# Strassen block products in the gated product of a two-layer trunk, with weight sums on VectorE and GpSimd

## Chip, cores and metric

The kernel runs on one core of a Trainium2 chip. TensorE (PE in the profile) multiplies, VectorE (DVE), ScalarE (ACT) and GpSimd (POOL) work elementwise, SyncE (SP) issues most DMAs. The metric is the device time of one execution in microseconds (us); lower is better. Each engine takes its instructions in an order of its own, and engines wait for one another by semaphores.

## What is computed

Two layers on an input of 256 positions by 2048 channels, float32. The first layer (a Mamba-2 mixer beside block-sparse attention) isn't touched. The second is a diagonal state-space mixer, and the change sits in its gated product, the line with `w_glu`:

```python
def s5_mixer(x, w_in, lam_re, ..., w_glu, w_out):
    u, gate = jnp.split(x @ w_in, 2, axis=-1)
    y = jax.nn.gelu(s5_ssm(u, lam_re, lam_im, log_dt, b_re, b_im, c_re, c_im, d_skip))
    ga, gb = jnp.split(y @ w_glu, 2, axis=-1)
    y = ga * jax.nn.sigmoid(gb)
    return (y * jax.nn.silu(gate)) @ w_out
...
        x = layer_norm(DEEPNORM_ALPHA * x + h, ln_g[layer], ln_b[layer])
```

Here `y` is 256 x 2048 and `w_glu` 2048 x 4096.

## The kernel before

**Products.** Every operand is split into a high and a low part, and a product takes three terms: high by high, high by low, low by high (xmm, L297 to L304). Weights come in units of two K tiles (128 rows each) by 512 columns, 512 KB: split_to loads a unit (L242, SP's queue, tile "raw"), ScalarE copies it to the rounded high half (L248, "wh"), VectorE subtracts to get the low half (L253, "wl"). Each of these tiles has four buffers, and split_to runs three units ahead of the matmuls, so the copy of unit n can start only when the matmuls of unit n - 4 are done. A unit is 2 K tiles x 2 halves of the 256 positions x 3 terms = 12 matmuls of 128x512.

**Gated product.** The 4096 columns are cut into 8 chunks of 512 (256 of ga, the matching 256 of gb), each of 16 K tiles, 8 units, 96 matmuls into two PSUM banks ("main"), one for each half of the positions. Two pairs of banks alternate. The operand is y5, the scan's output, whose K tiles lie in slot "A" in high and low form. Chunks 0 and 1 are made together by product_pair (L376): six units of chunk 0, six of chunk 1, then `between` (which finishes the scan's remaining jobs), then the last two units of chunk 0 (units 12 and 13 of the pair) and of chunk 1 (14 and 15). This is so because the last quarter of y5 comes late: y_load(3) (L1403, a reload from DRAM on GpSimd's DMA queue) and y_split(3) (L1413 and L1414) stand right ahead of it. The other six chunks follow one by one (`product`).

**After a chunk.** glu_jobs queues a gate job and a turn job. Gate: sigmoid of the gb half out of PSUM (L1455, ScalarE), product with the ga half (L1457, VectorE, twice 256 columns), product with the silu gate sg1 (L1458). Turn: four transposes on TensorE (L463 in a helper, tile "turn"), then the high and low halves of the next operand y2 (L1466 ScalarE, L1467 VectorE) in slot "C". Jobs are spread over the units that follow (pump, L282), and each one is held behind the splits of the unit two further on (run, L267).

**Around it.** Ahead stands the state-space scan, whose short matmuls and elementwise work are mixed into products with x1; it uses tiles of a pool (`w1`). Behind stands the output product with y2 (`wo1`), the residual with x1, and the layer norm. The order of instructions on each engine is worked out when the kernel is built, from the order of the code, these holds and the tile framework's scheduler.

## Time and profile before

| what | us |
|---|---|
| median of 3 runs (lowest to highest) | 1319.52 (1318.27 to 1320.66) |
| span of the profiled execution | 1316.6 |
| TensorE busy in it | 1310.0 |
| VectorE, ScalarE, GpSimd busy | 963.7, 695.5, 320.1 |
| gated product and what is mixed into it | about 1040 to 1229 |
| one chunk of it (96 matmuls, 4 transposes) | 22.23 |

In the rows of the profile a line such as `L253 DVE TENSOR_TENSOR wl<-raw,wh 128x1024 fp32r<-128x1024 f32 x430 | 532.8, 1243 | 284.1 <-ACT wh L248 282.1` gives the line of the code, the engine, the operation, the tile written and those read, shapes, the count, busy us in all, mean ns of one, idle us ahead of them on that engine, and who ended most of that idle time. In a timeline the first two numbers of a row are its start and its duration in us, x3 says that three instructions are merged, and the brackets give the idle time ahead and who ended it. Duration rows overlap a little, since an instruction begins before the one ahead has drained.

### The profile page before, as it was taken

The numbers are of one execution on the slowest core, as the hardware profiler recorded it, in microseconds if no ns is written. First come the engines' busy times: TensorE is split into PE (matmuls) and PEld (weight loads), VectorE is DVE, ScalarE is ACT, GpSimd is POOL, SyncE is SP. The second block draws the span as 40 slices with busy tenths as digits, with TensorE's granted clock in tenths as the row PEclk, the third lists the DMA queues.
The fourth block names the chain that finished last, engine by engine and source line by source line (L and its number), as shares of the span: only waits on it lengthen the run. The fifth ranks groups of instructions, "written<-read, shape, count | busy, mean of one in ns | idle before, by whom it ended". The sixth has DMA issues, their size and how long they took to land.

```text
span 1316.6 us, 21451 instructions
## 1 busy us (share of the span) xinstructions
PE 1310.0 (99%) x7999; PEld 1101.0 (84%) x7999; DVE 963.7 (73%) x1612; ACT 695.5 (53%) x946; POOL 320.1 (24%) x615
## 2 busy tenths in 40 slices
PE   9999999999999999999999999999999999999998
PEld 9988888878888888888888888888888888888885
DVE  6778977875786876777798765858998855555565
ACT  6566668865644554654654444444446544444441
POOL 0043000111045535236788300023232000000000
PEclk9999999999999999999999999999999999999999
DMA  8555566565556567666656868479998665555761
GB/s 318 181 181 178 187 208 194 192 206 176 175 177 239 200 217 230 203 207 225 229 201 231 285 219 312 153 246 320 332 288 311 211 217 191 189 192 188 255 224 68
DMA packets 96638, 288.33 MB, mean 219 GB/s; under 512 B 18994, under 2 KB 29186, under 8 KB 96020
## 3 DMA queue, kind: packets, MB, share of 16 engines
q1 hardware_dynamic: 75796, 245.05, 55.2%
q0 software_dynamic: 6336, 28.35, 6.3%
q10 hardware_dynamic: 14400, 13.54, 3.2%
q8 instruction: 63, 1.03, 0.3%
q14 instruction: 43, 0.35, 0.1%
HBM read 264.35 MB, written 21.00 MB: 217 GB/s over the span
## 4 chain that ended last, share of the span: by engine, by line
PE 99%; DVE 0%; ACT 0%; issue 0%
PE main L302 62%; PE main L358 17%; PE main L359 9%; PE main L325 3%; PE aux L463 2%; PE aux L917 1%; PE aux L818 1%; PE enc L1336 1%; PE dec L1381 1%; PE aux L1035 1%; PE aux L1003 1%; PE main L405 1%; PE dec L1377 0%; PE turn L463 0%; PE aux L472 0%; PE aux L1002 0%
## 5 line engine op out<-in xcount | busy, mean ns | idle before, releaser
L253 DVE TENSOR_TENSOR wl<-raw,wh 128x1024 fp32r<-128x1024 f32 x430 | 532.8, 1243 | 284.1 <-ACT wh L248 282.1
L248 ACT ACTIVATE wh<-raw 128x1024 fp32r<-128x1024 f32 x430 | 453.7, 1059 | 495.3 <-PE main L302 265.2
L302 PE MATMUL main<-wh,A 128*128 128x512 f32 x1536 | 488.0, 394 | 0.0
L302 PEld LDWEIGHTS main<-wh,A 128*128 128x128 f32 x1536 | 287.4, 188 | 59.5 <-issue 0.5
L302 PE MATMUL main<-wl,A 128*128 128x512 f32 x768 | 300.6, 391 | 0.0
L358 PE MATMUL main<-A,wh 128*128 128x512 f32 x768 | 272.7, 399 | 0.0
L302 PE MATMUL main<-wh,C 128*128 128x512 f32 x832 | 262.6, 393 | 0.0
L359 PE MATMUL main<-A,wl 128*128 128x256 f32 x768 | 215.3, 280 | 0.0
L302 PEld LDWEIGHTS main<-wh,C 128*128 128x128 f32 x832 | 155.7, 188 | 33.1
L358 PEld LDWEIGHTS main<-A,wh 128*128 128x128 f32 x768 | 144.2, 188 | 34.9 <-ACT b L890 0.4
L302 PEld LDWEIGHTS main<-wl,A 128*128 128x128 f32 x768 | 144.3, 188 | 28.7 <-issue 0.2
L302 PE MATMUL main<-wl,C 128*128 128x512 f32 x416 | 162.2, 390 | 0.0
L359 PEld LDWEIGHTS main<-A,wl 128*128 128x128 f32 x768 | 145.0, 189 | 0.4 <-issue 0.2
L742 POOL TENSOR_TENSOR c<-c 128x8 f32<-128x8 f32 (+2 forms) x192 | 96.0, 518 | 27.4 <-DMA wb<-c 19.9
L302 PEld LDWEIGHTS main<-wl,C 128*128 128x128 f32 x416 | 78.1, 188 | 16.1
L358 PE MATMUL main<-C,wh 128*128 128x512 f32 x192 | 68.3, 400 | 0.0
L925 POOL TENSOR_TENSOR ssq<-ssq,c 128x256 f32<-128x256 f32 x16 | 18.2, 1138 | 163.3 <-ACT c L923 162.7
L359 PE MATMUL main<-C,wl 128*128 128x256 f32 x192 | 53.5, 281 | 0.0
L744 POOL TENSOR_TENSOR c<-c,c 128x4 f32<-128x4 f32 (+2 forms) x96 | 49.2, 513 | 7.4
L976 POOL TENSOR_TENSOR b<-b 128x128 f32<-128x128 f32 x16 | 8.3, 518 | 172.2 <-DVE b L975 169.8
L745 POOL TENSOR_TENSOR c<-c,c 128x4 f32<-128x4 f32 (+2 forms) x96 | 47.2, 491 | 0.0
L358 PEld LDWEIGHTS main<-C,wh 128*128 128x128 f32 x192 | 36.0, 188 | 8.6
(298 smaller groups left out, 1344.4 us busy)
## 6 DMA issues: line engine op xcount, KB each, us to landing
raw<-in_wi SPq DMA_DIRECT2D x270, 512.0 KB
raw<-in_wo SPq DMA_DIRECT2D x96, 512.0 KB
raw<-in_wglu SPq DMA_DIRECT2D x64, 512.0 KB
wt<-wb POOLq DMA_DIRECT2D x16, 896.0 KB, 8.3
wb<-ob ACTq DMA_DIRECT2D x16, 512.0 KB
b<-cumd SPq DMA_DIRECT2D x16, 256.0 KB
bc<-in_s5bc SPq DMA_DIRECT2D x16, 256.0 KB
wb<-c POOLq DMA_DIRECT2D x16, 256.0 KB, 3.6
```

The costliest lines, as they stand in the source:

```text
L248: high = A.activation(wh, raw, AF.Copy)
L253: splits[n] = (loaded[-1], high, V.tensor_tensor(wl, raw, wh.bitcast(F32), op=OP.subtract))
L302: end = T.matmul(ps[o], l[:, k, sl], r[:, j, :], start=start and i == 0, stop=stop and i == 2)
L325: T.matmul(pv[o // 2][:, o % 2, :], l[:, j, sl], r[:, k, :], start=first and i == 0 and o % 2 == 0, stop=end and i == 2 and o % 2 == 1, sk ...
L358: T.matmul(ps[o], wh[:, j, sl], xx[:, k, :, :].rearrange("p a n -> p (a n)"), start=first, stop=False, skip_group_check=True)
L359: lastmm[:] = [T.matmul(ps[o][:, S : 2 * S], wl[:, j, sl], xh[:, k, :], start=False, stop=end, skip_group_check=True)]
L405: lastmm[:] = [T.matmul(pv[o // 2][:, o % 2, :], l[:, n, sl], r[:, k, :], start=at == 0 and l is wh and i == 0 and o % 2 == 0, stop=False, ...
L463: end = T.transpose(dst[:, i * P : i * P + P], s, ident)
L742: G.tensor_tensor(p[:, :, :, 0:m], cs[:, :, :, 1 : m + 1], cs[:, i, :, n : n + 1].unsqueeze(1).to_broadcast([P, 2, 4, m]), op=OP.mult)
L744: G.tensor_tensor(cs[:, 0, :, n + 1 : n + 1 + m], p0[:, 0, :, 0:m], p1[:, 1, :, 0:m], op=OP.subtract)
L745: G.tensor_tensor(cs[:, 1, :, n + 1 : n + 1 + m], p0[:, 1, :, 0:m], p1[:, 0, :, 0:m], op=OP.add)
L925: G.tensor_tensor(ssq, ssq, jk[:, f, :], op=OP.add)
```

## The change

Chunks 0 and 1 stay as they were. Chunks 2 to 7 are made in three pairs. In a pair, of the 16 K tiles six (0, 1, 2 and 4, 5, 6) are multiplied by Strassen's scheme in Winograd's form: the 2x2 blocks are the two halves of the positions by the two sets of three K tiles on one side, and the two sets of K tiles by the two chunks on the other. Seven products of 3 K tiles x 3 terms = 9 matmuls take the place of eight. The ten other K tiles are added as ordinary units (n1 for one chunk, n2 for the other) into the same PSUM banks, so a pair has 7 x 9 + 10 x 12 = 183 matmuls, where it had 2 x 96 = 192.

- The weight blocks a, b, c, d of a pair (128 x 1536 each, 768 KB) are loaded on SP's queue into tiles "sraw" (four buffers). Three sums t1, t2, t4 are made by VectorE in one more buffer, t3 by GpSimd in place. split_fast splits the seven operands into "sh" (ScalarE) and "sl" (VectorE), two buffers each.
- The operand sums of y5 (n1, n2, s3, n4) are made once, in `between`: two quarters of y are reloaded from DRAM (GpSimd's queue) into two buffers of "sraw", GpSimd adds, ScalarE and VectorE split.
- The block products p1, q5, v2, q7, p2, p4, p3 run in the order of `flow`, mixed with the units n1 and n2. Partial results are copied out of PSUM (copy, less, out1, out2).
- A gate then works on a whole chunk in SBUF: sigmoid on ScalarE, product with sg1 on GpSimd, the last product on VectorE (glu_whole).
- The tiles for this lie in a pool "gp", which is opened when the scan's pool "ws" is closed, in `between`. sg1 moves to slot "D", where x1 was; x1 is stored to DRAM (xkeep) ahead of the scan and reloaded behind the gated product.
- The bytes of weights loaded don't change. PSUM banks: the pair's first bank names X and Y are those of chunk 0 for the first pair, Z and R those of chunk 1.

Where lines are new, the numbers of the code after are used: L302 becomes L365, L248 L312, L253 L317, L1455 L1534, L1457 L1536, L1458 L1537, L1413 and L1414 L1481 and L1482.

```diff
+Q = 3
+KA = [0, 1, 2]
+KB = [4, 5, 6]
+KC = [3, 7, 8, 9, 10, 11, 12, 13, 14, 15]
+GROUPS = 3
...
+        flow = ["p1", "q5", "n2", "v2", "n2", "q7", "n2", "p2", "n1", "n2", "p4", "n1", "n2", "p3", "n1", "n1", "n1"]
+        fast = {}
+        before = {}
+        nc1 = len(KC) // 2
+        for g in range(GROUPS):
+            seen = {"n1": nc1, "n2": 0}
+            base = len(units)
+            for i, s in enumerate(flow):
+                if s in seen:
+                    units.append(io["wgc"][2 * nc1 * g + seen[s]])
+                    seen[s] += 1
+                else:
+                    fast[base + i] = (g, {"p1": "a", "q5": "t", "v2": "t", "q7": "b", "p2": "d", "p4": "t", "p3": "c"}[s])
+                    units.append(None)
+            at0 = {s: base + flow.index(s) for s in ("p1", "q5", "v2", "q7", "p4")}
+            for n, what in ((at0["p1"] - 1, ("load", "a")), (at0["p1"] - 1, ("load", "b")), (at0["p1"], ("load", "c")),
+                            (at0["q7"], ("load", "d")), (at0["p1"], ("sum", "t1")), (at0["q5"], ("sum", "t3")),
+                            (at0["v2"] - 1, ("sum", "t2")), (at0["p4"] - 1, ("sum", "t4"))):
+                before.setdefault(n, []).append((g,) + what)
...
+        gpool = []
+        blocks = {}
+
+        def block(g, name):
+            blocks[g, name] = gpool[0].tile([P, Q, 512], F32, tag="sraw", bufs=4, name=nm("sraw"))
+            return blocks[g, name]
+
+        def prepare(g, kind, name):
+            if kind == "load":
+                ins = nc.sync.dma_start(block(g, name).rearrange("p k n -> p (k n)"), io["wgs"][g, "abcd".index(name)])
+                blocks[g, name, "load"] = ins
+                loaded.append(ins)
+            elif name == "t1":
+                V.tensor_tensor(block(g, "t"), blocks[g, "a"], blocks[g, "b"], op=OP.add)
+            elif name == "t3":
+                G.tensor_tensor(blocks[g, "b"], blocks[g, "b"], blocks[g, "c"], op=OP.add)
+            else:
+                V.tensor_tensor(blocks[g, "t"], blocks[g, "t"], blocks[g, {"t2": "c", "t4": "d"}[name]], op=OP.add)
+
+        def split_fast(n):
+            raw = blocks[fast[n]]
+            wh = gpool[0].tile([P, Q, 512], F32R, tag="sh", bufs=2, name=nm("sh"))
+            high = A.activation(wh, raw, AF.Copy)
+            wl = gpool[0].tile([P, Q, 512], F32R, tag="sl", bufs=2, name=nm("sl"))
+            low = V.tensor_tensor(wl, raw, wh.bitcast(F32), op=OP.subtract)
+            splits[n] = (loaded[-1], high, low)
+            ready[n] = (wh, wl)
 
         def split_to(i):
             while nsplit[0] <= min(i, len(units) - 1):
                 n = nsplit[0]
+                for what in before.get(n, ()):
+                    prepare(*what)
+                if n in fast:
+                    split_fast(n)
+                    nsplit[0] += 1
+                    continue
...
+            scan = l1.enter_context(ExitStack())
+            ws = scan.enter_context(tc.tile_pool(name="ws", bufs=2))
 
             def w1(tag, shape, bufs=2, dt=F32):
-                return wk.tile(shape, dt, tag=tag, bufs=bufs, name=nm(tag))
+                return (wk if tag in ("p1", "gt") else ws).tile(shape, dt, tag=tag, bufs=bufs, name=nm(tag))
+
+            xkeep = dram.tile([P, 2, D], F32, name="xkeep")
+            jobs.append(lambda: nc.gpsimd.dma_start(xkeep, x1))
...
-            sg1 = wk.tile([P, 2, D], F32, tag="sg1", bufs=1, name="sg1")
+            sg1 = big("D", [P, 2, D])
...
+            def glu_whole(cc, j):
+                d = {}
+
+                sb, t1 = cc[:, :, 256:512], cc[:, :, 0:256]
+                d["t"] = t1
+
+                def gate():
+                    A.activation(sb, sb, AF.Sigmoid)
+                    G.tensor_tensor(sb, sb, sg1[:, :, 256 * j : 256 * j + 256], op=OP.mult)
+
+                def mix():
+                    V.tensor_tensor(t1, t1, sb, op=OP.mult)
+
+                return [gate, rest, mix, lambda: glu_turn(d, j)]
...
+            def between():
+                finish()
+                scan.close()
+                gpool.append(l1.enter_context(tc.tile_pool(name="gp", bufs=1)))
+                ops = gpool[0].tile([P, 4, 2, Q, P], F32R, name="ops")
+                xo["c1"] = gpool[0].tile([P, 2, 512], F32, name="c1")
+                ys = [gpool[0].tile([P, 4, S], F32, tag="sraw", bufs=4, name=nm("yr")) for _ in range(2)]
+                for i in range(2):
+                    nc.gpsimd.dma_start(ys[i], yd[i].rearrange("g a c -> (g a c)").rearrange("(f p t) -> p f t", p=P, t=S))
+
+                def tok(i, t):
+                    return ys[i].rearrange("p f (s t c) -> p t f s c", s=4, t=2)[:, t, 0:Q]
+
+                def put(name, i, tag, a, b, op):
+                    def go():
+                        a_, b_ = (xo[v, "r"] if isinstance(v, str) else tok(*v) for v in (a, b))
+                        r = xo[name, "r"] = w1(tag, [P, 2, 256]).rearrange("p a n -> p (a n)")[:, 0 : Q * P].rearrange("p (f s c) -> p f s c", f=Q, s=4)
+                        G.tensor_tensor(r, a_, b_, op=op)
+                        h, l = (ops[:, i, n].rearrange("p f (s c) -> p f s c", s=4) for n in range(2))
+                        A.activation(h, r, AF.Copy)
+                        V.tensor_tensor(l, r, h.bitcast(F32), op=OP.subtract)
+                        xo[name] = ops[:, i, 0], ops[:, i, 1]
+                    return go
+
+                jobs.extend([put("n1", 0, "gt", (0, 1), (1, 1), OP.subtract), put("n2", 1, "p1", "n1", (0, 0), OP.subtract),
+                             put("s3", 2, "gt", (0, 0), (0, 1), OP.subtract), put("n4", 3, "p1", "n2", (1, 0), OP.add)])
...
+                def copy(name, tag, ps):
+                    def go():
+                        e[name] = w1(tag, [P, 2, 256]).rearrange("p a n -> p (a n)")
+                        A.activation(e[name], ps, AF.Copy)
+                    return go
+
+                def less(o):
+                    A.activation(c2[:, o, :], X, AF.Copy)
+                    G.tensor_tensor(c2[:, o, :], e["z5"], c2[:, o, :], op=OP.subtract)
+
+                def out2():
+                    for o, ps in enumerate((Z, R)):
+                        V.tensor_tensor(c2[:, o, :], ps, c2[:, o, :], op=OP.add)
+
+                def out1():
+                    V.tensor_tensor(c1[:, 0, :], Y, e["p1"], op=OP.add)
+                    A.activation(c1[:, 1, :], X, AF.Copy)
+
+                made = {"p1": (X, lambda: whole(KA, 0), True, [copy("p1", "p1", X)]), "q5": (Y, lambda: summed("n1"), True, [copy("z5", "gt", Y)]),
+                        "v2": (X, lambda: summed("n2"), False, [lambda: less(0)]),
+                        "q7": (X, lambda: summed("s3"), False, [lambda: less(1)]),
+                        "p3": (Z, lambda: summed("n4"), False, [out2]), "p2": (Y, lambda: whole(KB, 0), True, []),
+                        "p4": (X, lambda: whole(KB, 1), False, [])}
+                for i, s in enumerate(flow):
+                    split_to(base + i + 3)
+                    wh, wl = ready.pop(base + i)
+                    if s in nn:
+                        ps = (Z, R) if s == "n2" else (Y, X)
+                        at = nn[s]
+                        nn[s] += 1
+                        end = i == len(flow) - 1
...
+                        ps, ops, start, after = made[s]
+                        for k, (h, l) in enumerate(ops()):
+                            for m, (a, b) in enumerate(((h, wh), (h, wl), (l, wh))):
+                                lastmm[:] = [T.matmul(ps, a, b[:, k, :], start=start and k + m == 0, stop=False, skip_group_check=True)]
+                    unit[0] += 1
+                    for f in after:
+                        run(f)
+                    if s == "p3":
+                        jobs.extend(glu_whole(c2, 3 + 2 * g))
+                    pump(len(flow) - 1 - i)
+                jobs.extend(glu_whole(c1, 2 + 2 * g))
+
+            product_pair(y5hl, between, glu_jobs)
+            names = [f"m{(turnno[0] - 1 + i // 2) % 2}{i % 2}" for i in range(4)]
+            for g in range(GROUPS):
+                product_fast(g, *[main.tile([P, 512], F32, tag=n, name=nm("main")) for n in names])
+                names = [names[2], names[3], names[1], names[0]]
+            turnno[0] += 1
...
+            x1 = big("D", [P, 2, D])
+            nc.gpsimd.dma_start(x1, xkeep)
```

Three places of the engines' order. The first is ScalarE's, from y_split(3) at the end of the pair product to the gate of chunk 0. Before (wh 11237 to 11291 are the pair's units 12 to 15, 11309 and 11327 the next chunk's first two):

```order
L1413 ACTIVATE A_9996<-ut_11193 128x4x128 x2
L248 ACTIVATE wh_11237<-raw_11235 128x1024
L248 ACTIVATE wh_11255<-raw_11253 128x1024
L248 ACTIVATE wh_11273<-raw_11271 128x1024
L248 ACTIVATE wh_11291<-raw_11289 128x1024
L248 ACTIVATE wh_11309<-raw_11307 128x1024
L248 ACTIVATE wh_11327<-raw_11325 128x1024
L1455 ACT_TABLE_LOAD
L1455 ACTIVATE gt_11343<-main_10986 128x256
```

After (11242, 11260, 11278, 11310 are the pair's units 12 to 15; sraw_11304 is block a, sraw_11344 the sum t1; 11398 to 11519 are the first four ordinary units):

```order
L312 ACTIVATE wh_11260<-raw_11258 128x1024
L269 ACTIVATE sh_11346<-sraw_11304 128x1536
L312 ACTIVATE wh_11278<-raw_11276 128x1024
L312 ACTIVATE wh_11310<-raw_11308 128x1024
L312 ACTIVATE wh_11398<-raw_11396 128x1024
L1580 ACTIVATE ops<-gt_11326 128x384
...
L1580 ACTIVATE ops<-p_1799_11338 128x384
L312 ACTIVATE wh_11519<-raw_11517 128x1024
L269 ACTIVATE sh_11363<-sraw_11344 128x1536
L1534 ACT_TABLE_LOAD
L1534 ACTIVATE gt_11379<-main_10991 128x256
```

The high half of block a now stands between the pair's units 13 and 14, and the sigmoid of chunk 0 behind the high half of t1. wh 11519 is the fourth unit behind the pair's unit 15, so it takes that one's buffer.

The second place is VectorE's at the same point, from unit 13 to the gate product of chunk 0 (L1457, L1536). Before:

```order
L253 TENSOR_TENSOR wl_11257<-raw_11253,wh_11255 128x1024
L253 TENSOR_TENSOR wl_11275<-raw_11271,wh_11273 128x1024
L253 TENSOR_TENSOR wl_11293<-raw_11289,wh_11291 128x1024
L253 TENSOR_TENSOR wl_11311<-raw_11307,wh_11309 128x1024
L253 TENSOR_TENSOR wl_11329<-raw_11325,wh_11327 128x1024
L1457 TENSOR_TENSOR p_1798_11344<-main_10986,gt_11343 128x256
```

After:

```order
L317 TENSOR_TENSOR wl_11262<-raw_11258,wh_11260 128x1024
L271 TENSOR_TENSOR sl_11348<-sraw_11304,sh_11346 128x1536
L317 TENSOR_TENSOR wl_11280<-raw_11276,wh_11278 128x1024
L317 TENSOR_TENSOR wl_11312<-raw_11308,wh_11310 128x1024
L317 TENSOR_TENSOR wl_11400<-raw_11396,wh_11398 128x1024
L1581 TENSOR_TENSOR ops<-gt_11326,ops 128x384
...
L260 TENSOR_TENSOR sraw_11344<-sraw_11304,sraw_11306 128x1536
L317 TENSOR_TENSOR wl_11479<-raw_11475,wh_11477 128x1024
L1581 TENSOR_TENSOR ops<-p_1799_11338,ops 128x384
L317 TENSOR_TENSOR wl_11521<-raw_11517,wh_11519 128x1024
L271 TENSOR_TENSOR sl_11365<-sraw_11344,sh_11363 128x1536
L1536 TENSOR_TENSOR p_1807_11380<-main_10991,gt_11379 128x256
```

Between unit 13's low half and the gate product there were four instructions; now there are thirteen (at the "..." stand the low half of one more unit and of two operand sums). t1 is written into a buffer that held a reloaded quarter of y, so it waits for GpSimd's last operand sum, which reads it.

The third is GpSimd's, which had no work in the gated product:

```order
L1569 DMA yr_11300<-yd_8735 128x4x256
L1569 DMA yr_11301<-yd_8736 128x4x256
L1578 TENSOR_TENSOR gt_11326<-yr_11300,yr_11301 128x384
L1578 TENSOR_TENSOR gt_11334<-yr_11300 128x384
L1578 TENSOR_TENSOR p_1797_11330<-gt_11326,yr_11300 128x384
L1578 TENSOR_TENSOR p_1799_11338<-p_1797_11330,yr_11301 128x384
L262 TENSOR_TENSOR sraw_11306<-sraw_11306,sraw_11342 128x1536
```

It reloads two quarters of y, makes the four operand sums, and then t3 of the first pair out of b and c (sraw 11306 and 11342). Loads of block a and b stand in SP's row right behind that of the pair's unit 15, and c's behind five ordinary units'.

More of the change, by code (lines that the diff above doesn't have):

```diff
@@ L295, in banks, with xmm @@
             return [main.tile([P, 512], F32, tag=f"m{turnno[0] % 2}{o}", name=nm("main")) for o in range(2)]
[L297 removed]
+        def xmm(ps, o, wpair, j, hk, start, stop, free=False):
             (xh, xl, xx), k = hk
@@ L301, in xmm @@
             for i, (l, r) in enumerate(((xh, wh), (xh, wl), (xl, wh))):
-                end = T.matmul(ps[o], l[:, k, sl], r[:, j, :], start=start and i == 0, stop=stop and i == 2)
+                end = T.matmul(ps[o], l[:, k, sl], r[:, j, :], start=start and i == 0, stop=stop and i == 2, skip_group_check=free)
             lastmm[:] = [end]
@@ L1469, in glu_jobs @@
-                rest = lambda: None
-                jobs.extend([gate, rest, rest, turn])
+                jobs.extend([gate, rest, rest, lambda: glu_turn(d, j)])
+            def glu_whole(cc, j):
[8 more added lines that the diff above has]
+                return [gate, rest, mix, lambda: glu_turn(d, j)]
```

52 lines of the change are left out of this document (36 added, 16 removed).

## Prediction

> **What bounds the kernel now.** I read the page's busy shares first, then the chain of work that ended last, then TensorE's waits.
>
> ```profile
> span 1316.6 us, 21451 instructions
> PE 1310.0 (99%) x7999; PEld 1101.0 (84%) x7999; DVE 963.7 (73%) x1612; ACT 695.5 (53%) x946; POOL 320.1 (24%) x615
> ...
> 1096.32 21.79 PE main L302 x96
> 1118.11 0.44 PE turn L463 x4
> 1118.55 21.82 PE main L302 x96
> ...
> PE aux L472 <- DVE idle L467: 1.0, 1, 1.0
> PE flip L1514 <- ACT pair L1513: 0.7, 1, 0.7
> PE sum L1517 <- ACT rowp L1515: 0.4, 1, 0.4
> ```
>
> The last three rows are all the waits of TensorE in the whole span (us in total, times, longest): 2.1 us, at the start and the end. Between them TensorE never waits for another engine. In the gated product the chain is one matmul after another: 96 of 512 columns in 21.79 us are 0.227 us each, and four transposes are 0.44. So a matmul taken away there is worth 0.227 us, and every us for which TensorE has to wait there is lost in full. Both signs are to be added up.
>
> ```profile
> core 0: us, PE busy (x) PEld busy (x) DVE busy (x) ACT busy (x) POOL busy (x), PEclk, DMA share, GB/s
> 1096.32:1118.55 22.23, 22.23 (x101) 18.42 (x101) 12.32 (x13) 10.03 (x13) 0.00 (x0) 1.00 0.56 190
> ```
>
> In one chunk of 22.23 us VectorE works 12.32, ScalarE 10.03, GpSimd nothing, and the DMAs are at 0.56. The work that the change adds to these three engines has room on the average. What is to be found is a place where it has none.
>
> **Term 1, matmuls.** A pair of chunks now takes 7 products of 3 K tiles by 3 terms (63 matmuls of 512) and 10 units of 12 (120): 183 where it was 192. Over three pairs 27 go, at 0.227 us: **-6.1 us**. The transposes stay as many.
>
> **Term 2, the way into the first pair.** Here the order of the engines decides, shown ahead of this prediction. The first matmul of the Strassen product p1 writes the PSUM bank of chunk 0, so it waits for chunk 0's gate product on VectorE (L1457 before, L1536 after). That one stood ahead of the end of the pair product; now 13 VectorE instructions stand between it and the low half of the pair's unit 13, the first of which is the low half of weight block a, and a's load cannot be issued until the scan's tiles are released, that is until y_split(3) is done.
>
> ```profile
> 1069.16 1.29 DVE L1414 TENSOR_TENSOR A<-ut,A 128x512 fp32r<-128x512 f32 x2 [4.06 <-ACT A L1413]
> 1070.63 3.50 DVE L253 TENSOR_TENSOR wl<-raw,wh 128x1024 fp32r<-128x1024 f32 x3 [0.17 <-ACT wh L248]
> ...
> 1081.89 0.76 DVE L1457 TENSOR_TENSOR p<-main,gt 128x256 f32<-128x256 f32 x2 [0.47 <-ACT gt L1455]
> ...
> 1077.09 1.06 ACT L248 ACTIVATE wh<-raw 128x1024 fp32r<-128x1024 f32 x1 [2.37 <-DMA raw<-in_wglu]
> 1079.10 1.06 ACT L248 ACTIVATE wh<-raw 128x1024 fp32r<-128x1024 f32 x1 [0.95 <-PE main L302]
> 1080.18 1.28 ACT L1455 ACT_TABLE_LOAD   x1
> ...
> 1084.54 1.06 ACT L248 ACTIVATE wh<-raw 128x1024 fp32r<-128x1024 f32 x1 [1.46 <-PE main L302]
> ...
> L242 SPq DMA_DIRECT2D raw<-in_wglu x6: 327/328/328, 1071.9 to 1081.5; - x6
> ...
> 1076.00:1080.00 4.00, 4.00 (x19) 3.34 (x18) 1.23 (x1) 1.96 (x2) 0.00 (x0) 1.00 0.79 302
> ```
>
> Start us, duration, engine. y_split ends at 1070.45 (1069.16 + 1.29). SP's first load behind it goes out at 1071.9 and its ScalarE copy starts at 1077.09, held by the load: 5.2 us for 512 KB. Block a has 768 KB, and b and two reloads of y (2.5 MB in all with a) go out at the same time; that stretch already moved 302 GB/s. Between 5.2 and 1.5 x 5.2 = 7.8 us I take 6.8: a lands at 1077.3. The pair product ends just before 1084.54, where ScalarE's copy had waited for it; I take 1084.4.
>
> The durations by shape:
>
> ```profile
> L248 ACT ACTIVATE wh<-raw 128x1024 fp32r<-128x1024 f32 x430 | 453.7, 1059 | 495.3 <-PE main L302 265.2 <-PE main L358 83.4 <-issue 42.4
> L1413 ACT ACTIVATE A<-ut 128x512 fp32r<-128x512 f32 x8 | 4.6, 626 | 4.7 <-DMA ut<-yd 4.7
> L253 DVE TENSOR_TENSOR wl<-raw,wh 128x1024 fp32r<-128x1024 f32 x430 | 532.8, 1243 | 284.1 <-ACT wh L248 282.1
> L1414 DVE TENSOR_TENSOR A<-ut,A 128x512 fp32r<-128x512 f32 x8 | 5.5, 710 | 5.1 <-ACT A L1413 5.1
> L1457 DVE TENSOR_TENSOR p<-main,gt 128x256 f32<-128x256 f32 x16 | 6.0, 417 | 0.5 <-ACT gt L1455 0.5
> L1455 ACT ACTIVATE gt<-main 128x256 f32<-128x256 f32 x16 | 5.1, 372 | 0.0
> ```
>
> From 512 to 1024 elements ScalarE adds 0.433 us and VectorE 0.533, so 1536 elements are estimated at 1.49 and 1.78. VectorE's 384 lie between 0.417 and 0.710: 0.56. Splits of 1024 back to back are 3.50 / 3 = 1.17. Block a's high half is ready at 1077.3 + 1.5 = 1078.8. From there VectorE's row: a's low half 1.78; three splits 3.5; one operand low half 0.56; a split 1.17; two low halves 1.12; the sum t1 1.78; a split 1.17; a low half 0.56; a split 1.17; t1's low half 1.78; the first gate product 0.42. Together **15.0 us**, to 1093.8. Units 14 and 15 of the pair product stand still in it, since their own splits are queued behind block a on ScalarE and VectorE; this is a part of the same delay, not another one.
>
> Into this row falls the new GpSimd work: four operand sums of 384 elements, on which VectorE's low halves and t1 wait, and the sum t3 of 1536.
>
> ```profile
> 639.93 0.57 POOL L742 TENSOR_TENSOR c<-c 128x64 f32<-128x64 f32 x2
> ...
> 641.12 1.78 POOL L742 TENSOR_TENSOR c<-c 128x128 f32<-128x128 f32 x2
> ...
> 643.86 1.38 POOL L742 TENSOR_TENSOR c<-c 128x248 f32<-128x248 f32 x2
> ...
> 641.40 1.23 DVE L253 TENSOR_TENSOR wl<-raw,wh 128x1024 fp32r<-128x1024 f32 x1 [3.10 <-ACT wh L248]
> ...
> 647.11 1.47 DVE L253 TENSOR_TENSOR wl<-raw,wh 128x1024 fp32r<-128x1024 f32 x1
> ```
>
> From 64 to 248 elements two additions grow by 0.81 us, 2.2 ns an element for one; so 384 are 0.99, 512 are 1.27 and 1536 are 3.5, and the five here 7.5 us. The pair of 128 should take 0.85. It took 1.78, more than the pair of 248, and the reader sees what lay beside it: a VectorE split of 1.23 us, so three quarters of the split (0.93 of 1.23) were lost to GpSimd. A later split (647.11) took 1.47 beside a GpSimd addition. Bounds: nothing, if they overlap wholly, and 7.5, if they exclude each other. I take three quarters, 5.6: p1 starts at 1099.4, **+15.0 us** after the pair's end (ends +9.4 and +16.9; less if a lands early, see the third rival).
>
> The Trainium skill, in "SBUF — State Buffer" under the heading on who interferes with whom, states that a VectorE instruction with two SBUF inputs and a GpSimd instruction that reads SBUF contend for a shared port pair, and that the later one blocks for the other's whole instruction. By that the sum takes all 7.5, +16.9, and a time 1.9 us above mine; the split at 641.40 shows three quarters of it.
>
> **Term 3, the clock after the stall.**
>
> ```profile
> 1309.00:1310.00 1.00, 0.64 (x3) 0.36 (x3) 0.96 (x3) 0.27 (x1) 0.00 (x0) 1.00 0.00 0
> 1310.00:1311.00 1.00, 1.00 (x3) 0.44 (x2) 0.96 (x3) 0.41 (x1) 0.00 (x0) 0.62 0.00 0
> 1311.00:1312.00 1.00, 1.00 (x2) 0.00 (x0) 0.76 (x1) 0.22 (x1) 0.00 (x0) 0.50 0.76 295
> ...
> 1306.60 0.02 issue
> ...
> 0.99 3.78 PE L472 MATMUL aux<-idle 128*128 128x512 f32 x8 [0.99 <-DVE idle L467]
> ```
>
> The dense matmuls end at 1306.6, and the granted clock falls from 1.00 to 0.62 and 0.50 in the stretches from 1310 on. At the start of the run, out of idleness, eight matmuls of 512 take 3.78 us, 0.47 each instead of 0.227: 1.9 us lost. A stall of 15 us in front of p1, most of it in one piece, should bring the same: **+1.9** (0 if the stall falls into pieces under 4 us).
>
> **Term 4, all the rest: 0.** Per pair VectorE has ten splits (11.7), seven of 1536 and three sums (17.8), three products out of PSUM and two mixes (3.5), four turn copies of 0.62 (2.5): 35.5 us; GpSimd 3.5 + 4 x 1.27 = 8.6. TensorE has 183 x 0.227 + 0.88 = 42.4. While the two overlap even in part, TensorE stays the bound and hides them; the price without that cover is the second rival. ScalarE stays under VectorE. Storing x1 to DRAM lies under the scan's matmuls. Its reload (2 MB, POOL's queue behind two loads of lnr) has about a product of time until the first residual needs it; that residual is a VectorE instruction, and TensorE meets it only a chunk later. I take 0 of 0 to 4.
>
> **Sum.** -6.1 + 15.0 + 1.9 = +10.8, on the span 1327.4. The median of the runs shown, 1319.52, is 2.9 us above the profiled span; so **1330.3 us**.
>
> **Rivals.**
> 1. *VectorE and GpSimd overlap fully.* For it: the split at 641.40 took its usual 1.23, so the loss fell on GpSimd, whose t3 nobody awaits at once. Against it: the four operand sums are awaited. Then +9.4 + 1.9 - 6.1: 1324.7.
> 2. *The two exclude each other in the pairs too.* 35.5 + 8.6 = 44.1 against 42.4 of TensorE: 1.7 us a pair, 5.1 in all beside the main terms, and 3 to 4 at the end at most: 1335.4. Against it: 6 of VectorE's 35.5 read PSUM. It decides where both together pass 42.4.
> 3. *Not slower: the row on VectorE is done in time, and only ScalarE's order binds.* ScalarE's sigmoid of chunk 0 now stands behind the split whose buffer is free only when the pair product has ended (the row at 1084.54 shows such a wait). After it come 0.15 + 1.06, t1's copy 1.49, the table load 1.28, a sigmoid 0.37, the product 0.42: 4.8 us, and that is the least there is. -6.1 + 4.8 = -1.3: 1318.2. It decides if VectorE's row ends by 1089.2, 4.6 us before my value without GpSimd: block a would have to land near 1072.7, two us after its issue, or the 14 instructions (it among them) be done in 10.4. No row speaks for that.
> 4. *Faster by over 0.2%.* The whole of term 1 is kept, 1313.4, only if the gate product is ahead of the pair's end as before; the order forbids it.
>
> **How the numbers follow.** Forecast 0.45; rival 1 0.20; rival 2 0.20; rival 3 0.10; rival 4 0.05. The range reaches from rival 3 to rival 2 with what the reload may add: 1318 to 1338, some 0.85. 0.2% (2.6 us) is about what a measurement can tell from no change. Faster by more: rival 4, 0.05. Within it, up to 1322.2: rival 3 and the lower edge of rival 1, 0.16. Slower: 0.79.
>
> **What would show it.** Right: TensorE's waits show one large wait of p1's first matmul on the gate product, about 15 us, some 2 to 4 of it in unit 14; nothing in the pairs after; granted clock under 1.00 for about 4 us behind it; 27 matmuls fewer; the chunk pairs at 42.4 us. Wrong: block a landing well ahead of 1077; GpSimd's additions at 1 us with VectorE at its usual durations; waits of TensorE for low halves in the second and third pair; a wait for the reloaded x1 at the end.

## The result, and the profile after

| | us |
| --- | --- |
| before, median of 4 runs | 1318.94 (1318.27 to 1320.66) |
| after, median of 4 runs | 1334.30 (1332.49 to 1336.09) |
| ratio after : before | 1.0113, 95% interval 1.0097 to 1.0128 |
| span of the profiled execution, before and after | 1316.6 and 1334.0 (+17.4) |
| the profiled execution's own time, after | 1335.76 |

The change is slower by 1.1%. The prediction was 1330.3 with a range of 1318 to 1338: sign and range held, and the point was 4.0 us low. Of the four executions of after, two took 1332.49 and 1332.83 us at a mean granted clock of 0.994 and two, the profiled one among them, 1335.76 and 1336.09 at 0.991. The page of after begins:

```profile
span 1334.0 us, 21469 instructions
...
PE 1308.1 (98%) x7972; PEld 1098.4 (82%) x7972; DVE 1006.8 (75%) x1625; ACT 715.7 (54%) x962; POOL 361.8 (27%) x638
...
PEclk9999999999999999999999999999999988999999
```

TensorE has its 27 matmuls less (7972 for 7999), yet its busy time fell by 1.9 us and not by 6.1. Two digits of the clock row show the larger part of the reason: in slices 33 and 34, the start of the first pair, matmuls ran at a lower granted clock and took longer. A second, shorter place of this kind lies in the scan (the stretch from 905 below). The rest of the loss is idle time. TensorE's waits (us in total, times, longest):

```profile
PE main L1643 <- issue: 14.4, 1, 14.4
PE enc L1404 <- issue: 3.2, 2, 2.0
...
PE main L388 <- ACT wh L312: 0.5, 1, 0.5
...
PE main L468 <- ACT wh L300: 0.3, 1, 0.3
PE main L365 <- DVE wl L317: 0.3, 1, 0.3
```

The first row is p1's wait that the prediction put at 15.0. The second was not in it: a wait of the encoding matmuls in the scan, ahead of the gated product. Stretches of after (start and end, length, busy time and instructions of PE, PEld, DVE, ACT and POOL, then the granted clock, the DMA share and GB/s):

```profile
905.00:915.00 10.00, 8.00 (x109) 6.91 (x108) 8.72 (x14) 3.70 (x5) 1.75 (x3) 0.83 0.82 323
1085.00:1105.00 20.00, 5.54 (x24) 4.05 (x22) 16.83 (x14) 9.31 (x12) 9.52 (x5) 0.72 0.77 274
1105.00:1115.00 10.00, 9.85 (x33) 7.79 (x34) 6.65 (x8) 5.18 (x8) 0.00 (x0) 0.71 0.04 14
1115.00:1125.00 10.00, 10.00 (x48) 8.26 (x47) 9.04 (x10) 7.38 (x9) 2.67 (x2) 1.00 0.54 196
1153.37:1195.81 42.44, 42.44 (x192) 35.13 (x192) 36.15 (x30) 26.01 (x29) 10.96 (x5) 1.00 0.54 193
```

The last row is the second pair: 42.44 us with TensorE busy throughout. Nor does it wait in the first and third, so the pairs do what the change says. The costs lie at the entry into the first pair (TensorE busy 5.54 of 20 us from 1085, the clock at 0.72 and 0.71 until 1115 and back at 1.00 after) and in the scan (8.00 of 10 us from 905, the clock at 0.83). The chain of work at the entry, in order of time (start, us, what):

```profile
1076.91 0.74 POOL yr L1569
1077.65 11.04 DMA yr<-yd
...
1088.83 1.43 POOL gt L1578
...
1090.71 1.05 ACT wh L312
...
1091.79 1.35 DVE wl L317
...
1093.49 1.00 DVE ops L1581
...
1095.23 1.76 DVE sraw L260
...
1097.01 5.86 DMA sraw<-in_wgs
1102.87 2.29 issue
1105.15 6.97 PE main L1643 x18
```

It starts with the reload of y, not with block a; from there it runs through GpSimd's operand sums, VectorE's low halves and t1. The chain puts the 5.86 us behind t1 down to a load of a later block; what VectorE did in that time, ahead of t1's low half, shows in the timeline (start, us, engine, operation):

```profile
1097.38 4.01 POOL L262 TENSOR_TENSOR sraw<-sraw,sraw 128x1536 f32<-128x1536 f32 x1 [2.96 <-DVE sraw L260]
1098.04 3.77 DVE L1581 TENSOR_TENSOR ops<-p,ops 128x384 fp32r<-128x384 f32 x1
...
1102.87 1.75 DVE L271 TENSOR_TENSOR sl<-sraw,sh 128x1536 fp32r<-128x1536 f32 x1
1104.54 0.74 DVE L1536 TENSOR_TENSOR p<-main,gt 128x256 f32<-128x256 f32 x2
```

A low half of 384 elements took 3.77 us and ended at 1101.81, 0.4 us after GpSimd's t3 (1097.38 + 4.01 = 1101.39). A split follows on VectorE, then t1's low half (L271) and the gate product (L1536), on which p1 waits.

The terms side by side, in us on the span:

| | predicted | measured |
| --- | --- | --- |
| 27 matmuls fewer | -6.1 | -6.1 |
| wait of p1, with unit 14's | +15.0 | +14.4 and about +0.3 |
| lower clock behind it | +1.9 | +2.9 |
| scan (storing x1) | 0 | +5.1 |
| start of the run | 0 | +0.7 |
| pairs, reload of x1 | 0 | 0 |
| sum | +10.8 | +17.3 of +17.4 |

The row on the clock: 18 matmuls took 6.97 us where 18 x 0.227 is 4.1. The row on the scan: y_split(3) ended at 1070.45 before and at 1076.29 after, 5.84 later, of which 0.7 are there from the run's first microseconds on: the waits of 0.3 and 0.5 us for ScalarE's splits, at 7 and 12 us. The change edits nothing there, and the other profiles are between 0.2 early and 1.0 late at this place, so this row is scatter. The waits in the scan that the profile names are 3.2; of the other 1.9, 1.7 are the matmuls at a clock of 0.83 in the ten us from 905, and the rest lies in pieces too small to name.

### The profile page after: what moved, and what is told of

It reads as the page before. It is cut to its first block, busy times and chain, and to the rows that moved or that the text cites. A ratio compares the mean times of both kernels' runs of the same rounds, so it can differ in the third digit from the quotient of the medians.

```text
span 1334.0 us, 21469 instructions
## 1 busy us (share of the span) xinstructions
PE 1308.1 (98%) x7972; PEld 1098.4 (82%) x7972; DVE 1006.8 (75%) x1625; ACT 715.7 (54%) x962; POOL 361.8 (27%) x638
## 4 chain that ended last, share of the span: by engine, by line
PE 96%; DMA 2%; issue 1%; DVE 0%; ACT 0%; SPq 0%; POOL 0%; POOLq 0%
PE main L365 56%; PE main L421 17%; PE main L422 9%; PE main L1643 3%; PE main L388 3%; PE aux L526 2%; DMA yr<-yd 1%; PE aux L980 1%; PE enc L1404 1%; PE aux L881 1%; PE dec L1449 1%; PE aux L1098 1%; PE aux L1066 1%; DMA raw<-in_wi 1%; PE dec L1445 0%
## 5 line engine op out<-in xcount | busy, mean ns | idle before, releaser
L317 DVE TENSOR_TENSOR wl<-raw,wh 128x1024 fp32r<-128x1024 f32 x412 | 515.1, 1254 | 241.4 <-ACT wh L312 238.1
L312 ACT ACTIVATE wh<-raw 128x1024 fp32r<-128x1024 f32 x412 | 434.0, 1059 | 454.4 <-PE main L365 215.5
L365 PE MATMUL main<-wh,A 128*128 128x512 f32 x1392 | 444.2, 394 | 0.0
L365 PEld LDWEIGHTS main<-wh,A 128*128 128x128 f32 x1392 | 260.2, 188 | 53.7 <-issue 0.5
L365 PE MATMUL main<-wl,A 128*128 128x512 f32 x696 | 272.7, 392 | 0.3 <-DVE wl L317 0.3
L365 PE MATMUL main<-wh,C 128*128 128x512 f32 x832 | 261.9, 393 | 0.0
L365 PEld LDWEIGHTS main<-wh,C 128*128 128x128 f32 x832 | 155.4, 188 | 32.9
L365 PE MATMUL main<-wl,C 128*128 128x512 f32 x416 | 162.3, 390 | 0.0
L365 PEld LDWEIGHTS main<-wl,A 128*128 128x128 f32 x696 | 130.8, 188 | 27.0 <-DVE wl L317 0.7
L365 PEld LDWEIGHTS main<-wl,C 128*128 128x128 f32 x416 | 78.1, 188 | 16.3
L271 DVE TENSOR_TENSOR sl<-sraw,sh 128x1536 fp32r<-128x1536 f32 x21 | 38.9, 1850 | 20.0 <-ACT sh L269 16.3
```

The lines of the kernel that those rows point to most:

```text
L271: low = V.tensor_tensor(wl, raw, wh.bitcast(F32), op=OP.subtract)
L312: high = A.activation(wh, raw, AF.Copy)
L317: splits[n] = (loaded[-1], high, V.tensor_tensor(wl, raw, wh.bitcast(F32), op=OP.subtract))
L365: end = T.matmul(ps[o], l[:, k, sl], r[:, j, :], start=start and i == 0, stop=stop and i == 2, skip_group_check=free)
```

## Experiments

Each kernel is the changed one with the edit shown. The kernel before took 1318.5 to 1319.1 us (medians) on the same chips; ratios are to it.

**1. The store of x1 left out.** (e1_no_store) Two theories for the 5 us in the scan: the bytes of the store, or its place in a queue. Here the store is gone and the reload reads as many bytes of the input.

```diff
-            xkeep = dram.tile([P, 2, D], F32, name="xkeep")
-            jobs.append(lambda: nc.gpsimd.dma_start(xkeep, x1))
...
-            nc.gpsimd.dma_start(x1, xkeep)
+            for i in range(2):
+                nc.gpsimd.dma_start(x1[:, i, :].rearrange(...), io["xn"][:, :, i, :].rearrange(...))
```

> The store of x1 to DRAM is left out and the reload reads rows of the input instead (same bytes), so the output is not the reference's. In the profile of after, TensorE was 5.7 us late before the gated product began (y_split(3) ended at 1076.29 instead of 1070.45), with waits of 3.2 us in front of the scan's first matmuls. Theory 1 (the 2 MB store at 852 us holds back the loads ahead of the scan): y_split(3) ends within 1.5 us of 1070.5, no wait of the scan's matmuls, and 1329 us (1328 to 1331). Rival (the lateness comes from the scan's tiles being in a pool of their own, or from run to run): it stays, 1332 to 1336 us.

Measured: 1333.49 us, ratio 1.0111 (1.0096 to 1.0126). The wait of the encoding matmuls is gone, as the expectation has it; the time is not, and y_split(3) still ends at 1074.94, 4.5 us later than before. Of these, 3.5 are there ahead of the scan. p1's wait is 15.2, and 1.7 us of TensorE went elsewhere, at about 705 us (busy 18.29 of the 20 us from 700), in a stretch where the order of the instructions is that of the kernel before. ScalarE there waits longer for a transfer (the wait stands in the brackets; this kernel first, then before):

```profile
705.34 0.81 ACT L897 ACTIVATE om<-moved,consts 128x128 f32<-128x128 f32 x2 [6.59 <-DMA moved<-kt]
```

```profile
701.62 1.34 ACT L834 ACTIVATE om<-moved,consts 128x128 f32<-128x128 f32 x3 [3.90 <-DMA moved<-kt]
```

A stall of TensorE at this place, of 1.0 to 2.3 us, is in the profiles of experiments 1, 3, 6, 8 and 9 (0.3 in 10), and in none of before, after, 2, 4, 5, 7 and 11; experiments 1, 2, 4 and 6 ran on one chip, two with it and two without. Why the transfer is late there was not tried.

**2. The store in two parts.** (e2_store_parts) If a long transfer is what stands in the way, two short ones should cost less.

```diff
-            jobs.append(lambda: nc.gpsimd.dma_start(xkeep, x1))
+            for cols in (slice(0, 1536), slice(1536, D)):
+                jobs.append(lambda cols=cols: nc.gpsimd.dma_start(xkeep[:, :, cols], x1[:, :, cols]))
```

> The same store in two parts: 1.5 MB go out as soon as those columns of x1 are final (842.5 us, where the DMAs are nearly idle until 855), 0.5 MB at 852. Theory 1 in the form that the moment counts: most of the 5.7 us come back, 1329 to 1331.5 us. Rival (the bytes count, whenever they are moved, or the queue does): 1333 to 1336 us.

Measured: 1336.12 us, 1.0134 (1.0117 to 1.0152): no better than after, by the medians worse. Each part is one more entry of `jobs`, and each entry takes one turn of the list that also holds the copies of u for the scan. ScalarE makes 287 copies of weight units ahead of the first of those copies before, 288 after, and 289 here. That speaks for the place.

**3. The store without a turn.** (e5_store_direct) The same bytes on the same queue of GpSimd, issued at once instead of from the list.

```diff
-            jobs.append(lambda: nc.gpsimd.dma_start(xkeep, x1))
+            nc.gpsimd.dma_start(xkeep, x1)
```

> The whole store of x1 as in the changed kernel, but issued on GpSimd's queue without taking a turn in the queue of jobs, where it pushed the scan's first job (the copies of u out of PSUM, L1344) behind one more unit. In the run without the store those copies stood where they do in the kernel before, and the scan's matmuls did not wait. Theory 1b (the turn in the job queue costs the scan its 3.2 us of waits and some 1.7 us at a lower clock): no wait of the scan's matmuls, 1329 to 1331 us. Rival (the bytes moved at 852 us cost it): waits of 2 to 4 us stay, 1332 to 1336 us.

Measured: 1332.88 us, 1.0107 (1.0093 to 1.0120). No wait of the encoding matmuls is left, with all bytes stored. Two groups of matmuls, transposes just ahead of the scan and the scan's last decoding matmuls, in before, after and this kernel:

```profile
852.65 0.60 PE L463 MATMUL aux<-consts,D 128*128 128x128 f32 x4
...
1051.68 0.41 PE L1381 MATMUL dec<-gt,wt 64*64 64x63 f32 x16
```

```profile
853.33 0.60 PE L526 MATMUL aux<-consts,D 128*128 128x128 f32 x4
...
1057.43 0.41 PE L1449 MATMUL dec<-gt,wt 64*64 64x63 f32 x16
```

```profile
854.53 0.60 PE L526 MATMUL aux<-consts,D 128*128 128x128 f32 x4
...
1053.58 0.41 PE L1449 MATMUL dec<-gt,wt 64*64 64x63 f32 x16
```

Between the two groups lie 199.03 us before, 204.10 after and 199.05 here: the 5.1 us of the scan are gone in full. The 1.9 us by which this kernel is still late at the scan's end were there ahead of it; TensorE's stall at 705 us (busy 18.96 of the 20 us from 700) stands in that part. The other profiles agree: experiments 4 and 5, which keep the turn, have 202.95 and 202.43 us between the two groups, and experiment 1, without it, 198.99. So it was the turn in the list, which moved the scan's first copies by a unit, and not the bytes; nor is it the scan's own pool of tiles, the rival of experiment 1, which this kernel keeps. Its price is 3.4 to 5.1 us; the largest is that of after, where the clock fell behind the first wait (0.83 in the ten us from 905; 1.00 there in experiments 4 and 5). The whole time gained less than that, 1.4 us, and is 2 us above the expectation: beside that stall, p1's wait rose from 14.4 to 15.2 and low halves are waited for.

**4. The gate product not held behind the splits.** (e3_gate_free) `run` holds every job of the list behind the splits of the units already due. Here the gates are exempt.

```diff
-                for ins in splits.get(min(unit[0] + 2, nsplit[0] - 1), ()):
+                for ins in () if job in free else splits.get(min(unit[0] + 2, nsplit[0] - 1), ()):
...
+                free.add(gate)
                 jobs.extend([gate, rest, rest, lambda: glu_turn(d, j)])
```

> The gates of chunks 0 and 1 are no longer held behind the splits of the unit two further on; chunk 0's gate product then stands ahead of t1's low half and of the last operand sum on VectorE, at about 1097 us instead of 1104.5. Theory 2 (the row of sums behind the reload of y is what holds, the gate is only its last link): p1 starts some 7 us earlier but q5 then waits for t1's low half, and 2 to 3 us are gained: 1331 to 1332.5 us. Rival (the place of the gate is the cause): 7 us or more are gained, 1325 to 1328 us.

Measured: 1332.95 us, 1.0118 (1.0089 to 1.0146; one of the four executions took 1340.35), which by the time alone can't be told from after. Its profile can:

```profile
PE main L1646 <- issue: 7.4, 1, 7.4
...
PE main L1646 <- DVE sl L271: 1.7, 1, 1.7
```

p1 starts after 7.4 us, half of the wait. Then the next product, q5, waits for the low half of t1, which is where VectorE's row ends, and the granted clock stays at 0.50 for 12.3 us from p1's start (5.7 us in after). From the scan's last decoding matmuls to the end this profile is 2.6 us shorter than after's, of 7.0 us of wait saved. So half of p1's wait was only the place of the gate behind t1, but most of what is saved there is lost again: with the gate freed, the next thing late is t1 itself.

**5. t3 on VectorE.** (e8_t3_dve) The sum on GpSimd beside which a low half took 3.77 us.

```diff
-                G.tensor_tensor(blocks[g, "b"], blocks[g, "b"], blocks[g, "c"], op=OP.add)
+                V.tensor_tensor(blocks[g, "b"], blocks[g, "b"], blocks[g, "c"], op=OP.add)
```

> The changed kernel with the sum t3 on VectorE instead of GpSimd. In the profile of after, VectorE's low half of the last operand sum (384 elements) took 3.77 us beside t3 on GpSimd (1536 elements, 4.01 us) and ended with it. Theory 3 (the two exclude each other for a whole instruction): the low half takes 0.5 us; t3 costs VectorE 1.75 instead of the 3.3 lost, so p1 starts about 1.5 us earlier or t3 moves behind the gate altogether and p1 starts 3 us earlier: 1331 to 1333 us. Rival (VectorE's row is simply longer by t3): 1335 to 1337 us.

Measured: 1333.17 us, 1.0117 (1.0102 to 1.0133), again not to be told from after by the time. In its profile the low half is short, and p1 waits 12.8 us, not 14.4:

```profile
1095.78 0.55 DVE L1581 TENSOR_TENSOR ops<-p,ops 128x384 fp32r<-128x384 f32 x1
...
1097.39 1.75 DVE L262 TENSOR_TENSOR sraw<-sraw,sraw 128x1536 f32<-128x1536 f32 x1
```

The same low half takes 0.55 us without GpSimd beside it. VectorE now does t3 itself, in 1.75 us where GpSimd took 4.01, and still ends earlier: 0.55 + 1.75 is less than 3.77. From the scan's last decoding matmuls to the end this profile is 1.3 us shorter than after's.

**6. The operand sums in the scan, early.** (e4_sums_early) The reload of y, the four sums and their halves after y_split(1), far ahead of the product; the reload of the second quarter is spared, since y_split(1) has it.

```diff
+                    if b == 7:
+                        at(2 * b + 11, y_sums)
...
-                for i in range(2):
-                    nc.gpsimd.dma_start(ys[i], yd[i].rearrange(...))
...
-                jobs.extend([put("n1", 0, "gt", (0, 1), (1, 1), OP.subtract), ...
```

> The four operand sums of y are made during the scan, right after y_split(1), from a reload of quarter 0 and the quarter 1 that is there; the reloads at the start of the first pair and GpSimd's four sums there are gone. Theory 2 (the reload of 11 us and the sums behind it are the wait): p1 starts 2 to 4 us after the pair product's end instead of 15, the clock does not drop, 1317 to 1321 us. Rival (VectorE's row of splits alone fills the gap, as the prediction's 9.4 us without GpSimd had it): 1326 to 1329 us.

Measured: 1332.76 us, 1.0099 (1.0077 to 1.0121). The expectation was missed by far. At the entry TensorE waits 5.2 us instead of 14.7 (1.9 + 0.6 + 2.6), but the scan gave it back:

```profile
PE enc L1407 <- issue: 6.4, 3, 2.7
PE main L365 <- DVE wl L317: 4.2, 3, 1.9
PE main L1647 <- DVE sl L271: 2.6, 1, 2.6
```

Of the second row, 2.3 us are the stall at 705 us. GpSimd issues the scan's loads, and the reload and the sums stand in its row ahead of them; that this is what costs the scan is read from the order of the rows, and the next experiment moves them.

**7. The operand sums at the end of the scan.** (e6_sums_late) The same, behind GpSimd's last copy of a table, with a tile for y that the weight pool holds, so that blocks a and b are not held by y_split(3).

```diff
+                put("n1", 0, y1[1], y0[1], y1[1], OP.subtract)
...
+                    with tc.issue_after(after[15].ins):
+                        G.tensor_tensor(r, a_, b_, op=op)
...
+            at(30, y_again)
+            at(34, y_sums)
```

> The operand sums are made during the scan as in the run before, but behind GpSimd's last instruction for the scan, where they hold back none of its loads; and the tile of the reloaded y is apart from the scan's pool, so that blocks a and b can be loaded before y_split(3). Theory 2: p1 starts within 3 us of the pair product's end, the scan's waits are those of the changed kernel (3.2 us, store as it was), 1317 to 1321 us. Rival (VectorE's row, the reload taken away, still holds p1 for 9 us): 1325 to 1329 us.

Measured: 1326.01 us, 1.0053 (1.0039 to 1.0066): 8.3 us of after's loss gone with one move, though less than expected. The time lies in the range noted for the rival, but not by its mechanism: VectorE's row doesn't hold p1 any more, which starts without a wait at 1094.95. What is left:

```profile
PE enc L1407 <- issue: 4.3, 3, 1.8
PE main L365 <- DVE A L1485: 2.4, 1, 2.4
```

The second row is new. Blocks b and c now land early, so t3 starts early, and it falls beside the last low halves of y.

**8. Experiments 7, 3 and 4 together.** (e7_all)

> The two edits together (store outside the job queue; operand sums behind the scan's GpSimd work, blocks a and b ahead of y_split(3)), and the gates of chunks 0 and 1 not held behind splits. Theory: all waits of TensorE in the scan and at the first pair are gone or under 2 us, the 27 matmuls remain: 1312 to 1315 us, faster than the kernel before (1318.9) by 4 us or more. Rival (the 27 matmuls are given back in the pairs, since VectorE and GpSimd then hold them): 1317 us or more.

Measured: 1319.40 us, 1.0009 (1.0000 to 1.0017): about the time before, and above the expectation. That is the rival's range, but what it assumed, waits in the pairs, isn't in the profile. The encoding wait is down to 0.5 us. The largest left is the one on y's low halves, and its cause stands beside it:

```profile
1075.65 4.15 POOL L262 TENSOR_TENSOR sraw<-sraw,sraw 128x1536 f32<-128x1536 f32 x1 [8.22 <-DMA sraw<-in_wgs]
...
1076.38 4.57 DVE L1487 TENSOR_TENSOR A<-ut,A 128x512 fp32r<-128x512 f32 x2
...
1080.40 0.73 PE L367 MATMUL main<-wh,A 128*128 128x512 f32 x2 [2.36 <-DVE A L1487]
```

Two low halves that took 1.29 us before take 4.57, and the second ends after t3 does.

**9. Experiment 8 with t3 on VectorE.** (e9_all_t3_dve) The edit of 5 on top.

> The version with all edits, and t3 on VectorE. In the profile of that version with t3 on GpSimd, TensorE waited 2.4 us for y_split(3)'s low halves on VectorE (4.57 us for two instead of 1.29, beside t3, 4.15 us, on GpSimd), and the clock fell behind it (0.93 from 1060 to 1085). Theory 3 (VectorE and GpSimd exclude each other there): the two low halves take 1.3 us, this wait is under 0.5 us, the clock stays at 1.00: 4 us less, 1314.5 to 1317 us, faster than the kernel before (1318.5). Rival (the load of the last quarter of y, 8.5 us beside the loads of blocks a and b, is what TensorE waits for): 1318.5 to 1320 us.

Measured: 1318.66 us, 0.9993 (0.9984 to 1.0002). The two low halves are back at 1.29, as the theory has it, but the time gained only 0.7 us, with intervals that overlap. The profiled execution, at 1321.62 the longest of the eleven, waits 2.1 us for the encoding at 1036:

```profile
1029.96 2.66 DVE L1421 TENSOR_TENSOR p<-gt,wt 128x512 f32<-128x512 f32 x2
...
1031.06 1.00 POOL L1501 TENSOR_TENSOR y<-y,y 128x384 f32<-128x384 f32 x1
1032.14 1.35 POOL L1501 TENSOR_TENSOR y<-y 128x384 f32<-128x384 f32 x1
1032.65 1.13 DVE L1436 TENSOR_TENSOR gt<-p,p 128x256 f32<-128x256 f32 x1
1033.58 2.23 POOL L1501 TENSOR_TENSOR y<-y,y 128x384 f32<-128x384 f32 x2
1033.70 1.24 DVE L1437 SCALAR_TENSOR_TENSOR gt<-p,p 128x256 f32<-128x256 f32 x1
```

The same exclusion at another place: the four sums (L1501) now lie beside VectorE's recurrence of the scan, on which the next encoding waits.

**10. The operand sums on VectorE too** (e12_all_dve), behind the recurrence's last instruction; they enter the list of work one unit later, at 35 for 34.

```diff
-                    with tc.issue_after(after[15].ins):
-                        G.tensor_tensor(r, a_, b_, op=op)
+                    with tc.issue_after(after["r"].ins):
+                        V.tensor_tensor(r, a_, b_, op=op)
```

> The version with all edits and t3 on VectorE, and the four operand sums too on VectorE, behind its last instruction of the scan's recurrence. In the profile of the version before, the scan's matmuls waited 2.1 us at 1036, after VectorE's instructions of the recurrence had taken 2.66 instead of 1.29, 1.13 instead of 0.42 and 1.24 instead of 0.42 us beside GpSimd's operand sums (1031 to 1036). Theory 3 (exclusion): with no GpSimd addition left there, that wait and the lower clock behind it (0.99 from 925 to 1060) are gone, 2.5 to 3.5 us less: 1315 to 1316.5 us. Rival (the two reloads of y on GpSimd's queue hold the scan's own loads): the wait stays, 1318 to 1319.5 us.

Measured: 1317.70 us, 0.9988 (0.9980 to 0.9997), 1.2 us above the expected range. The recurrence's instructions are short again (L1421's pair 1.28, L1436 and L1437 0.43 and 0.42), and each of the four sums takes VectorE 0.55. One wait of 1.4 us is left, for the low half of the pair's unit 14, which stands behind t3.

**11. Experiment 10 with t3 behind that low half.** (e13_all_dve_pin)

```diff
-                V.tensor_tensor(blocks[g, "b"], blocks[g, "b"], blocks[g, "c"], op=OP.add)
+                with tc.issue_after(splits[starts[g] - 1][2].ins):
+                    V.tensor_tensor(blocks[g, "b"], blocks[g, "b"], blocks[g, "c"], op=OP.add)
```

> The same, with t3 held behind the low half of the pair product's last unit on VectorE, since TensorE waited 1.5 us at 1084 for the low half of unit 14 that stood behind t3 and t1's low half. If those 1.75 us are the wait, another 1 to 1.5 us go: 1314 to 1315.5 us, faster than the kernel before by 0.2% or more. Rival (the wait is that of the sums' loads, or moves to v2, which needs t2): within 0.5 us of the run without it.

Measured: 1316.62 us (1315.31 to 1317.75, 11 runs) against 1319.09 before on the same chip: ratio 0.9981 (0.9972 to 0.9990). That is above the expected 1314 to 1315.5. The gain over experiment 10 is 1.1 us by the medians; the intervals overlap and the profiled spans are equal (1314.7 and 1314.5), so this step alone isn't shown to gain. The version beats both kernels, by 2.5 us and by 17.7. Its page, and the waits of TensorE over 0.5 us that the kernel before doesn't have:

```profile
PE 1305.1 (99%) x7972; PEld 1094.9 (83%) x7972; DVE 1001.7 (76%) x1632; ACT 717.3 (55%) x962; POOL 349.4 (27%) x631
```

```profile
...
PE aux L530 <- DVE D L1208: 0.7, 1, 0.7
PE main L1653 <- DVE sl L273: 0.7, 1, 0.7
PE enc L1411 <- DMA wt<-wb: 0.6, 1, 0.6
PE main L369 <- DVE wl L319: 0.6, 2, 0.3
...
```

TensorE's busy time is 4.9 us under that before (1310.0 - 1305.1). Of that the span keeps 1.9 (1316.6 to 1314.7): most of the rest, 2.6 us, stands in these rows.

## Why the prediction was right, and where it was not

**What bounds the kernel** was read rightly: TensorE was never late before, so a matmul is worth its 0.227 us and every wait counts. **Term 1** came as forecast: a pair takes 42.44 us where two chunks took 2 x 22.23, 2.0 less. **Term 4** was right for the pairs: 42.44 us where 42.4 was worked out, VectorE 36.15 where 35.5, GpSimd 10.96 where 8.6. The second rival (the two exclude each other in the pairs, 44.1 us) fell: TensorE waits for nothing there, though the two engines' busy times add up to 47.1 us in 42.44. The busy time of an instruction that is held holds the wait too (3.77 us for one of 0.55 in after), so their sum counts some time twice.

**Term 2** has the right size, 14.4 and not 15.0, and the right place, but its inside was partly wrong. Block a landed sooner than I had it: its load went out at 1076.43 and its copy on ScalarE began at 1081.05, 4.6 us later and not 6.8. GpSimd was dearer: 1.00 to 1.86 us for a sum of 384 and 4.0 for t3, where I had 0.99 and 3.5. And the row did not start from block a at all, but from the reload of y, which takes 11 us to land and which I had put beside a's load without a price of its own. Two errors cancelled, and that is luck: the row's start came later, and it was shorter, since a's low half and three splits were done while VectorE waited for y. From the end of y_split to p1's start I had 1099.4 - 1070.45 = 28.95; it was 1105.15 - 1076.29 = 28.86. Experiments 6 and 7 show the reading of the place: with reload and sums out of this row, p1 itself waits 0.6 us (6) or not at all (7, where blocks a and b also land earlier).

That VectorE and GpSimd would delay each other, at three quarters of GpSimd's time, was the weakest number of the term. The runs settle it: beside t3 the low half took 3.77 instead of 0.55 (experiment 5), two of 512 took 4.57 instead of 1.29 (8 and 9), instructions of the recurrence took two to three times their time (9 and 10). In after, the VectorE instruction ends only after GpSimd's, by 0.4 us, less than its own length. This is not three quarters but the whole of what was left of the other's instruction, as the Trainium skill has it ("SBUF — State Buffer", the section on who interferes with whom). The first rival, full overlap, fell with it. What it cost in VectorE's row to p1 is 4.8 us, where I had 5.6: 3.2 beside t3, and 1.6 beside the operand sums, where two low halves took 0.79 and 1.35 for 0.55 and a split 1.78 for 1.21.

**Term 3** was too small by 1.0 in this execution: 6.97 us for 18 matmuls, +2.9 where I took +1.9 from the start of the run. The size varies. In experiment 1 p1 starts at 1104.64 behind a wait of 15.2 us, and the ten us from 1105, at 0.71 in after, are at 0.88:

```profile
1105.00:1115.00 10.00, 9.38 (x38) 7.34 (x38) 7.20 (x8) 6.12 (x8) 0.00 (x0) 0.88 0.02 7
```

There the nine matmuls of p1 took 3.65 us where 9 x 0.227 is 2.0, a loss of 1.6, and the clock was back at 1.00 behind them; experiment 2 has 3.69 us behind 14.4. So 1.9 lies between what was measured. That pieces under 4 us cost nothing, as the term has it, isn't borne out: the wait of 2.0 us at 906 in after has the stretch at 0.83 behind it, though one of 2.4 us at the same place in experiment 4 left the clock at 1.00. The Trainium skill ("TensorE: Matmul & The Clock Gate", Part 1) has TensorE at half speed for about 3.4 us of work after an idle window, an estimated loss of 1.7. Experiments 1 and 2 agree with that; after, with 5.7 us at a clock of 0.50 behind p1's wait, disagrees in size.

**The step that failed** is in term 4: "Storing x1 to DRAM lies under the scan's matmuls", costed at nothing. The transfer does. What I did not cost is that its issue is an entry of the list `jobs` and takes a turn ahead of the scan's copies of u, which moves them back by one unit. Experiment 3 shows it: same bytes, no turn, no wait of the encoding matmuls. In after the scan costs 5.1 us on the span for it, 3.2 in waits and most of the rest in the lower clock behind the first of them, the largest part of the 6.6 by which the span was missed (1334.0 for 1327.4). The step from span to time then took some of it back, by luck: I had added 2.9 us, of which an execution's own time has only 1.8 on top of its span (1335.76 for 1334.0), because the profiled execution before was shorter than its median; after, it is 1.5 longer than its median. So the time was missed by 4.0.

**Third and fourth rival**, no change or faster, fell as the prediction had it: neither VectorE's row nor the gate product was done in time. But the wait was a matter of order, not of the method: experiment 11 has the same 27 matmuls fewer and p1 at 1087.81 without a wait.

**Open.** What makes the transfer late and TensorE wait at 705 us in five of the experiments; why the clock stays low for 2.8 us of matmuls behind one long wait and 5.7 behind another; why the reload of y takes 11 us at the entry (as loads of 384 KB a piece, put into the scan, they land in 8.0); and whether the small waits of experiment 11 can go too, which would be worth up to another 2.6 us.

## What to carry to other kernels

Where one engine is never late, fewer instructions on it are worth at most their time, and the change is decided by the first place at which its inputs are made: follow that row to its very start, the reloads too, and ask which of them is last. Moving a sum to an idle engine is no gift if it reads the same memory beside a busy engine; here GpSimd's four sums and t3 took less time on VectorE, which was busy three quarters of the time, and moving them there brought 1319.40 us to 1317.70 (experiments 8 and 10). And an issue that costs nothing can still cost a turn in a list of work.

## What the runs showed of the hardware

- VectorE instructions with two inputs in SBUF did not overlap with GpSimd additions on SBUF: a low half of 0.55 us took 3.77 beside a GpSimd addition of 4.01, and two of 1.29 took 4.57 beside one of 4.15.
- An addition of 1536 elements took GpSimd 4.0 to 4.4 us and VectorE 1.75; one of 384 took 1.0 to 1.9 and 0.55.
- Behind the 14.4 us wait most of p1 and q5 ran at a lower granted clock: 0.50 for 5.7 us, 18 matmuls in 6.97 us instead of 4.1. Behind the 15.2 us wait of experiment 1 it was 0.50 for 2.8 us. A wait of 2.0 us at 906 had a stretch at 0.83 behind it, one of 2.4 us in experiment 4 had none.
- Reloading 2 x 512 KB on GpSimd's queue beside 2 x 768 KB on SP's took 11.0 us, while SP's first block took 4.6; the store of 2 MB took 6.6.
